# A streaming encoder step: the first layer norm written into TensorE's order among the last convolutions, the sums of both layer norms on VectorE, and the last two taps of a GpSimd convolution behind a gate

## The chip, the cores and the metric

The kernel runs on one core of a Trainium2 chip. The metric is the time of one execution on the device in microseconds (us). A core has five engines that each work through a fixed list of instructions in order: TensorE (PE in the profile, its weight loads PEld), VectorE (DVE), ScalarE (ACT), GpSimd (POOL) and SyncE (SP), which mostly issues DMAs. They wait for each other through semaphores. [...]

## The reference

One step of a small encoder for two groups of frames: 512 new frames of one stream and 16 new frames of each of 8 running streams, 640 columns together, with a model width of 1024. The first layer is a convolution module and a feed-forward network, the second an attention layer and a feed-forward network. The change lies in the convolution module:

```python
def layer_norm(x, g, b):
    xf = x.astype(jnp.float32)
    mu = jnp.mean(xf, axis=-1, keepdims=True)
    var = jnp.mean(jnp.square(xf - mu), axis=-1, keepdims=True)
    y = (xf - mu) * lax.rsqrt(var + EPS)
    return (y * g.astype(jnp.float32) + b.astype(jnp.float32)).astype(x.dtype)

def conv_module(h, hist, g, w_pw1, b_pw1, w_dw, b_dw, ln_g, ln_b, w_pw2, b_pw2):
    a, gate = jnp.split(rms_norm(h, g) @ w_pw1 + b_pw1, 2, axis=-1)
    glu = a * jax.nn.sigmoid(gate)
    full = jnp.concatenate([hist.astype(glu.dtype), glu], axis=1)
    y = lax.conv_general_dilated(full, w_dw[:, None, :], ..., feature_group_count=D_MODEL) + b_dw
    y = jax.nn.silu(layer_norm(y, ln_g, ln_b))
    return h + y @ w_pw2 + b_pw2, full[:, -CONV_HIST:]
```

The depthwise convolution has 31 taps. The layer norm takes its mean and its variance over the 1024 channels of each frame.

## The kernel before, in words

**Layout.** Channels lie on the 128 partitions in 8 blocks, frames in the free dimension: the 128 frames of the running streams first, then the 512 of the new one. The 640 columns are worked on as two groups of 320 (`g` is 0 or 1; `gr[g]` has start and width). Each matrix product is three matmuls with operands split into a rounded part and a rest (`mm3`, L179 to L181): weight-high by x-high, weight-low by x-high, weight-high by x-low. `wsplit` makes the weight parts (`whi` on ScalarE, L152, `wlo` on VectorE, L156), `xsplit` those of the operands (L168, L169).

**Order.** A string, `PLAN`, lists the steps of the module, and `step` emits each. A planner then puts every engine's instructions in order by priority and by modelled times, so that instructions of a later step can be put among those of an earlier one wherever they seem ready. `tc.issue_after(i)` ties the instructions emitted inside it that run on the engine of `i` to stand behind `i` on that engine; `tc.high_priority` raises priorities.

**The steps.** `a`, `b`, `c`, and the first half of `C` to `F` make the GLU of a channel block (`glu`, tanh at L717, the other half's copy at L720, the product on VectorE at L724 and L730). The convolutions of the eight blocks are spread over the engines. Step `q` (block 0, then block 3) is a GpSimd convolution of the new stream's 512 frames (`conv_pool`): for each of 31 taps ScalarE makes a product (`cvt`, L777, four buffers) and GpSimd adds it to `ca` (L780). Step `d` gives parts of blocks 0 to 2 to VectorE (`conv_taps`, L766 and L769), some of whose last taps are held for step `e`, behind E7's GLU. Blocks 4 to 7 are done by TensorE (`conv_pe`, L818) in three parts: `S` (the 128 frames), `A` (192 more, which with S fill group 0) and `B` (the 320 of group 1). A part is 8 tap groups of 4 matmuls; a matmul in plain float32 shows as two instructions in the trace, so a part has 64. Part B reads a copy of the data shifted by DMA (`xb`, two buffers, `conv_read`, L800); that of block 7 is read in step `L`. Each part ends in a copy from PSUM to `y` by ScalarE (`to_y`, L738); four PSUM banks (`mm`) go round among GLU halves and convolution parts. Step `k` copies the results of VectorE's and GpSimd's convolutions to `y`.

**The layer norms.** Step `n` is `conv_ln(g)`. The mean over channels is a matmul of each block of `y` with a column of 1/1024 (`colmean`, L216, three tiles of 128 frames, so 6 instructions an operand); the first `LCUT[g]` blocks are added first (on GpSimd, L207) into one operand. A small reduction (L220), a copy (L829) and a matmul (`spread`, L228) bring the mean back to all partitions; VectorE subtracts it from the eight blocks (L832), ScalarE squares them (L188, `sql`). The squares' mean goes the same way with `SQCUT[g]`: for group 0 all eight blocks go to TensorE, for group 1 GpSimd adds the eight first. EPS is added on VectorE (L250), the power -0.5 taken on GpSimd (L257), the result spread; VectorE multiplies (L841), ScalarE applies silu (L843), and `xsplit` makes the operands of `pw2`. Step `w` (`pw2`) is the last pointwise product, per group 4 pairs of output blocks with 24 matmuls an output. The feed-forward network (L404) follows.

Before, step `n0` stands ahead of `B5 L7 B6 B7` in the list and the planner mixes them on TensorE; `n1` stands behind.

Of the kernel before, what the change touches and what calls it, by code (L numbers as in the profile page):

```python
# [15 lines left out]
P = 128  # L16
# [7 lines left out]
T = 512  # L24
# [18 lines left out]
CUT, LCUT, SQCUT = 8, (5, 5), (1, 8)  # L43
# [25 lines left out]
        "S7 A7 n0 B5 L7 B6 B7 s0 n1 w0 w1")  # L69
# [9 lines left out]
def tile_trunk(ctx, tc, xT, vecs, hist, w_pw1, w_pw2, w_in0, w_out0, w_os0, w_in1, w_out1, w_os1,  # L79
# [96 lines left out]
    def mm3(ps, wts, xs):  # L176
        last = len(wts) - 1
        for i, ((wh, wl), (xh, xl)) in enumerate(zip(wts, xs)):
            nc.tensor.matmul(ps, wh, xh, start=(i == 0), stop=False)  # L179
            nc.tensor.matmul(ps, wl, xh, start=False, stop=False)  # L180
            end = nc.tensor.matmul(ps, wh, xl, start=False, stop=(i == last))  # L181
        return end
# [11 lines left out]
    def tiles(n):  # L194
        return [min(t, n - P) for t in range(0, n, P)]

    def colmean(st, pieces, n, cut, tag, eng=nc.gpsimd, accp=None):
# [15 lines left out]
        for k, f in enumerate(srcs):  # L213
            s = f()
            for t, a in enumerate(tiles(n)):
                nc.tensor.matmul(st[:, 512 + t * w + k:513 + t * w + k], s[:, a:a + P],  # L216
                                 onec, start=True, stop=True)
# [8 lines left out]
    def spread(st, r, n):  # L226
        for t, a in enumerate(tiles(n)):
            nc.tensor.matmul(st[:, a:a + P], r[:, t:t + 1].to_broadcast([P, P]), ident,  # L228
                             start=True, stop=True)
        return st[:, :n]  # L230
# [466 lines left out]
    glu_end, gate_end = [None], [None]  # L697
# [74 lines left out]
    def conv_pool(c):  # L772
        acc = cp.tile([P, T], F32, tag="ca", name=nm("ca"))
        for j in range(W):
# [6 lines left out]
        return lambda: to_y(c, NB * SB, T, acc, func=AF.Copy)  # L781
# [22 lines left out]
    def conv_pe(c, part):  # L804
# [3 lines left out]
        for tg in range(8):  # L808
            r = 96 if tg == 7 else P
            for q in range(4):  # L810
# [5 lines left out]
                else:  # L816
                    mv = xb[0:r, q, 4 * tg:4 * tg + n]
                nc.tensor.matmul(pt[32 * q:32 * q + 32, 0:n], w4[0:r, 4 * tg + q, :], mv,  # L818
                                 start=(tg == 0), stop=(tg == 7))
# [3 lines left out]
    def conv_ln(g):  # L823
# [3 lines left out]
        r, v = colmean(mu, [lambda c=c: y[g][:, c, :] for c in order], n, LCUT[g], "mst")  # L827
        if v is not r:
            nc.vector.tensor_copy(r[:, :len(tiles(n))], v)  # L829
        spread(mu, r, n)  # L830
        for c in order:
# [3 lines left out]
        bc, _ = rstd_bc([y[g][:, c, :] for c in order], n, SQ, SQCUT[g],  # L835
                        sqs=[sq[:, i, :] for i in range(KT)])
# [9 lines left out]
        return z  # L846

    def pw2(g, z):
        n = gr[g][1]
        for m2 in M2[g]:  # L850
# [3 lines left out]
            if m2 < 2:  # L854
                del pws[KT, m2]
            for i in range(2):
                m = 2 * m2 + i
                pt = mmt()
                mm3(pt[:, :n], [(wh[:, (i * 8 + k) * P:(i * 8 + k + 1) * P],
                                 wl[:, (i * 8 + k) * P:(i * 8 + k + 1) * P]) for k in range(KT)],  # L860
                    xk(z, range(KT)))
# [547 lines left out]
```

## Time and profile before

| | |
|---|---|
| runs | 1490.59, 1491.54, 1494.51 us |
| median | 1491.54 us |
| the profiled execution | 1494.89 us, its span 1493.1 us |
| mean granted TensorE clock | 0.988 |
| busy: TensorE, VectorE, ScalarE, GpSimd | 97%, 75%, 51%, 22% of the span |
| from the GLU of block 7 to the first pw2 matmul | 135.9 to 198.5 us |

The page lists busy times, groups of instructions and the chain that ended last. The timeline gives the start and the duration of each instruction or run of instructions, its engine, line, tiles and shape; a bracket says how long the engine was idle before it and who released it. In the windows the granted clock is 1.00 at full speed.

### The profile page before, as it was taken

The numbers are of one execution on the slowest core, as the hardware profiler recorded it, in microseconds if no ns is written. First come the engines' busy times: TensorE is split into PE (matmuls) and PEld (weight loads), VectorE is DVE, ScalarE is ACT, GpSimd is POOL, SyncE is SP. The second block draws the span as 40 slices with busy tenths as digits, with TensorE's granted clock in tenths as the row PEclk, the third lists the DMA queues.
The fourth block names the chain that finished last, engine by engine and source line by source line (L and its number), as shares of the span: only waits on it lengthen the run. The fifth ranks groups of instructions, "written<-read, shape, count | busy, mean of one in ns | idle before, by whom it ended". The sixth has DMA issues, their size and how long they took to land.

```text
span 1493.1 us, 28157 instructions
## 1 busy us (share of the span) xinstructions
PE 1443.9 (97%) x10998; PEld 1377.0 (92%) x10998; DVE 1125.9 (75%) x2494; ACT 757.4 (51%) x1620; POOL 325.5 (22%) x376
## 2 busy tenths in 40 slices
PE   5998999999999999999999999999999999999997
PEld 5997789999999999999988898878999999999997
DVE  5788546799788788766867668576788888788754
ACT  3666246464554554444655355443454455465443
POOL 5789322011111111013222111012001111111101
PEclk9999999999999999999999999999899999999998
DMA  7167514034544544424555554452024544544512
GB/s 238 67 169 199 117 57 140 31 101 121 156 110 118 153 112 116 145 86 157 195 175 193 178 193 163 142 186 78 29 75 118 148 117 115 151 117 108 157 58 71
DMA packets 66661, 192.57 MB, mean 129 GB/s; under 512 B 12000, under 2 KB 30176, under 8 KB 58080
## 3 DMA queue, kind: packets, MB, share of 16 engines
q1 hardware_dynamic: 52736, 161.10, 33.2%
q0 software_dynamic: 13504, 29.37, 9.7%
q8 instruction: 86, 1.41, 0.4%
q14 instruction: 47, 0.39, 0.1%
q10 hardware_dynamic: 288, 0.31, 0.1%
HBM read 179.14 MB, written 11.61 MB: 128 GB/s over the span
## 4 chain that ended last, share of the span: by engine, by line
PE 81%; POOL 6%; DVE 6%; ACT 4%; DMA 1%; issue 1%; POOLq 0%; DVEq 0%; ACTq 0%
PE mm L404 48%; PE mm L179 8%; PE mm L180 7%; PE mm L181 7%; POOL ca L780 5%; PE mm L818 2%; PE w L216 2%; PE am L1154 1%; PE w L1170 1%; PE am L1137 1%; ACT whi L144 1%; PE am L1201 1%; DVE wlo L338 1%; ACT whi L152 1%; DVE hid L558 1%
## 5 line engine op out<-in xcount | busy, mean ns | idle before, releaser
L404 PE MATMUL mm<-XH,whi 128*128 128x320 f32 x896 | 276.0, 311 | 1.1 <-ACT t L414 1.0
L404 PE MATMUL mm<-XH,wlo 128*128 128x320 f32 x896 | 277.0, 310 | 0.0
L404 PE MATMUL mm<-XL,whi 128*128 128x320 f32 x896 | 274.7, 309 | 0.0
L337 ACT ACTIVATE whi<-raw 128x512 fp32r<-128x512 f32 (+2 forms) x280 | 169.4, 613 | 146.2 <-PE mm L404 114.5
L179 PE MATMUL mm<-xh,whi 128*128 128x320 f32 (+2 forms) x640 | 201.0, 316 | 4.2 <-ACT xh L168 2.6
L338 DVE TENSOR_TENSOR wlo<-raw,whi 128x512 fp32r<-128x512 f32 (+2 forms) x280 | 184.9, 668 | 22.8 <-ACT whi L337 21.6
L180 PE MATMUL mm<-xh,wlo 128*128 128x320 f32 (+2 forms) x640 | 199.7, 313 | 0.6 <-DVE wlo L156 0.6
L181 PE MATMUL mm<-xl,whi 128*128 128x320 f32 (+2 forms) x640 | 196.8, 312 | 0.0
L404 PE MATMUL mm<-hid,whi 128*128 128x320 f32 x732 | 172.0, 310 | 2.9 <-DVE hid L338 2.6
L404 PEld LDWEIGHTS mm<-XH,whi 128*128 128x128 f32 x896 | 168.4, 189 | 2.1 <-ACT t L414 2.1
L404 PEld LDWEIGHTS mm<-XH,wlo 128*128 128x128 f32 x896 | 168.7, 188 | 0.0
L404 PEld LDWEIGHTS mm<-XL,whi 128*128 128x128 f32 x896 | 167.9, 188 | 0.0
L404 PEld LDWEIGHTS mm<-hid,whi 128*128 128x128 f32 x732 | 124.8, 188 | 5.8 <-DVE hid L338 3.7
L179 PEld LDWEIGHTS mm<-xh,whi 128*128 128x128 f32 x640 | 121.5, 190 | 7.4 <-ACT xh L168 3.1
L180 PEld LDWEIGHTS mm<-xh,wlo 128*128 128x128 f32 x640 | 121.7, 190 | 1.0 <-DVE wlo L156 0.8
L181 PEld LDWEIGHTS mm<-xl,whi 128*128 128x128 f32 x640 | 120.6, 189 | 0.4 <-issue 0.2
L404 PE MATMUL mm<-hid,wlo 128*128 128x320 f32 x366 | 112.9, 308 | 0.0
L404 PE MATMUL mm<-XH,shi 128*128 128x320 f32 x344 | 107.2, 312 | 3.2 <-ACT XH L337 3.2
L404 PE MATMUL mm<-XL,shi 128*128 128x320 f32 x344 | 106.8, 312 | 1.3 <-DVE XL L338 1.3
L404 PE MATMUL mm<-XH,slo 128*128 128x320 f32 x344 | 106.9, 311 | 0.0
L383 POOL DMA_DIRECT2D s<-in_w_in x38 | 22.0, 579 | 388.8 <-DVE wlo L338 208.6
L780 POOL TENSOR_TENSOR ca<-ca,cvt 128x512 f32<-128x512 f32 x60 | 91.4, 1524 | 15.0 <-ACT cvt L777 8.0
(245 smaller groups left out, 3389.1 us busy)
## 6 DMA issues: line engine op xcount, KB each, us to landing
raw<-in_w_in SPq DMA_DIRECT2D x38, 1024.0 KB
s<-in_w_in POOLq DMA_DIRECT2D x76, 256.0 KB, 4.2
raw<-in_w_os SPq DMA_DIRECT2D x24, 768.0 KB
cache<-in_ck SPq DMA_DIRECT2D x32, 512.0 KB
cache<-in_cv SPq DMA_DIRECT2D x32, 512.0 KB
raw<-in_w_pw SPq DMA_DIRECT2D x12, 1024.0 KB
s<-in_w_os POOLq DMA_DIRECT2D x48, 192.0 KB, 3.6
raw<-in_w_kq SPq DMA_DIRECT2D x8, 1024.0 KB
```

The lines of the kernel that those rows point to most:

```text
L144: nc.scalar.activation(out=hi[:, a:b], in_=raw[:, a:b], func=AF.Copy, scale=gain)
L152: nc.scalar.activation(out=hi[:, a:b], in_=raw[:, a:b], func=AF.Copy)
L179: nc.tensor.matmul(ps, wh, xh, start=(i == 0), stop=False)
L180: nc.tensor.matmul(ps, wl, xh, start=False, stop=False)
L181: end = nc.tensor.matmul(ps, wh, xl, start=False, stop=(i == last))
L216: nc.tensor.matmul(st[:, 512 + t * w + k:513 + t * w + k], s[:, a:a + P], onec, start=True, stop=True)
L337: nc.scalar.activation(out=hi, in_=src, func=AF.Copy)
L338: put_end[0] = nc.vector.tensor_tensor(out=lo, in0=src, in1=hi.bitcast(F32), op=sub).ins
L383: nc.gpsimd.dma_start(s1, src[:, 2 * n:3 * n])
L404: last = nc.tensor.matmul(pt, wt, v, start=(first and k == i == 0), stop=(k == n - 1 and i == 2), skip_group_check=True)
L780: nc.gpsimd.tensor_tensor(out=acc, in0=acc, in1=pr, op=ALU.add)
L818: nc.tensor.matmul(pt[32 * q:32 * q + 32, 0:n], w4[0:r, 4 * tg + q, :], mv, start=(tg == 0), stop=(tg == 7))
```

## The change

- **Order of the first layer norm.** Step `n` is now `staged_ln`. `conv_ln` has become a generator with stops, and `conv_pe` one that stops after each tap group. `staged_ln` runs them in turn, each tied behind the last TensorE instruction of the other: the mean behind A7; one tap group of B5; the spread of the mean, the subtractions, the squares and their sum; twelve tap groups (the rest of B5, the reading of block 7's copy, five of B6); the squares' mean; two tap groups; the spread of the power and the rest of the norm; then the nine groups left. Step `m` is the second layer norm.
- **Sums.** `LCUT` for group 0 goes from 5 to 7. The sums of the means of both norms are on VectorE instead of GpSimd; the squares of both norms are added into one operand on VectorE (before: none for group 0, on GpSimd for group 1). The second norm's mean sum is tied behind the first one's sum of squares on VectorE.
- **The gate.** Of the 31 taps of block 3's GpSimd convolution the last two (`QHELD`) are emitted in step `e`, their products on ScalarE tied behind the tanh of E7.
- **pw2.** The two outputs of a pair take their banks together, and for the first pair of group 0 the loop over the blocks of `z` is outside that over the two outputs.

```diff
-CUT, LCUT, SQCUT = 8, (5, 5), (1, 8)
+CUT, LCUT = 8, (7, 5)
+GAPS = 1, 12, 2
+QHELD = 2
-        "S7 A7 n0 B5 L7 B6 B7 s0 n1 w0 w1")
+        "S7 A7 n s0 m w0 w1")
...
+    def pool_taps(c, acc, js):
+        for j in js:
...
+    def conv_pool(c):
+        acc = cp.tile([P, T], F32, tag="ca", name=nm("ca"))
+        n = W - QHELD if c else W
+        pool_taps(c, acc, range(n))
+        return (lambda: to_y(c, NB * SB, T, acc, func=AF.Copy),
+                lambda: pool_taps(c, acc, range(n, W)))
...
-    def conv_ln(g):
+    def conv_ln(g, after=None):
         n = gr[g][1]
         mu = w2t()
         order = LNO[g]
-        r, v = colmean(mu, [lambda c=c: y[g][:, c, :] for c in order], n, LCUT[g], "mst")
+        with nullcontext() if after is None else tc.issue_after(after):
+            r, v = colmean(mu, [lambda c=c: y[g][:, c, :] for c in order], n, LCUT[g], "mst",
+                           nc.vector)
         if v is not r:
             nc.vector.tensor_copy(r[:, :len(tiles(n))], v)
-        spread(mu, r, n)
+        conv_end[0] = mean_end[0]
+        yield
+        end = spread(mu, r, n, True)
...
-        bc, _ = rstd_bc([y[g][:, c, :] for c in order], n, SQ, SQCUT[g],
-                        sqs=[sq[:, i, :] for i in range(KT)])
+        conv_end[0] = end
...
+            sum_end[0] = nc.vector.tensor_tensor(out=acc[:, :n], in0=prev, in1=s, op=ALU.add).ins
+            prev = acc[:, :n]
+        yield
+        r, v = colmean(st, [lambda: prev], n, 1, "rst", nc.vector)
...
+        nc.gpsimd.tensor_tensor(out=r2[:, :nt], in0=r[:, :nt], in1=mhalf[:, :nt], op=ALU.pow)
+        conv_end[0] = mean_end[0]
+        yield
+        conv_end[0] = spread(st, r2, n, True)
...
+    def last_convs():
+        yield from conv_pe(5, "B")
+        x4s[7][2] = x4s[7][2]()
+        yield from conv_pe(6, "B")
+        yield from conv_pe(7, "B")
+
+    def staged_ln():
+        ln, convs = conv_ln(0), last_convs()
+        for gap in GAPS + (None,):
+            with tc.issue_after(conv_end[0]):
+                next(ln, None)
+            with tc.issue_after(conv_end[0]):
+                for _ in convs if gap is None else range(gap):
+                    if gap is not None:
+                        next(convs)
...
+            pair = [mmt()[:, :n], mmt()[:, :n]]
+            both = m2 == M2[0][0] and g == 0
+            for ks in [range(k, k + 1) for k in range(KT)] if both else [range(KT)]:
+                for i in range(2):
+                    mm3(pair[i], [(wh[:, (i * 8 + k) * P:(i * 8 + k + 1) * P],
+                                   wl[:, (i * 8 + k) * P:(i * 8 + k + 1) * P]) for k in ks],
+                        xk(z, ks), ks[0] == 0, ks[-1] == KT - 1)
...
             with tc.issue_after(gate_end[0]):
                 conv_taps(held, {})
+            with tc.issue_after(glu_end[0]):
+                pool_rest.pop()()
```

More of the change, by code (lines that the diff above doesn't have):

```diff
@@ L224, in colmean, with spread @@
         return r, st[:, 512:512 + nt]
-    def spread(st, r, n):
+    def spread(st, r, n, ins=False):
         for t, a in enumerate(tiles(n)):
-            nc.tensor.matmul(st[:, a:a + P], r[:, t:t + 1].to_broadcast([P, P]), ident,
-                             start=True, stop=True)
-        return st[:, :n]
+            end = nc.tensor.matmul(st[:, a:a + P], r[:, t:t + 1].to_broadcast([P, P]), ident,
+                                   start=True, stop=True)
+        return end.ins if ins else st[:, :n]
     def rsqrt(y, v):
```

60 lines of the change are left out of this document (39 added, 21 removed).

## The prediction

> **What bounds the kernel now.** I read the page's busy row first, then the list of what TensorE waited for, then the timeline of TensorE between 118 and 221 us, then those of ScalarE, VectorE, GpSimd and the DMA queue beside it, and last the windows for the granted clock.
>
> ```profile
> span 1493.1 us, 28157 instructions
> PE 1443.9 (97%) x10998; PEld 1377.0 (92%) x10998; DVE 1125.9 (75%) x2494; ACT 757.4 (51%) x1620; POOL 325.5 (22%) x376
> ```
>
> TensorE is busy for 97% of the span, so the end moves by what TensorE is given less to do, by what it waits less, and by the clock at which it does it. All three occur between 143 and 221 us, and the change lies there.
>
> First place, the gate. Rows give start, duration, engine, line and count; the bracket is idle time and its releaser.
>
> ```profile
> 118.26 4.57 PE L818 MATMUL mm<-xa,w 128*32 128x128 f32 x128
> 131.45 4.52 PE L818 MATMUL mm<-xb,w 128*32 128x320 f32 x64
> 143.13 1.96 PE L818 MATMUL mm<-xa,w 128*32 128x128 f32 x64
> 148.09 4.14 PE L818 MATMUL mm<-xa,w 128*32 128x192 f32 x64 [3.00 <-ACT y L738]
> ```
> ```profile
> 141.92 1.32 ACT L777 ACTIVATE cvt<-gall,dwv 128x512 f32<-128x512 f32 x2
> 145.56 0.72 ACT L777 ACTIVATE cvt<-gall,dwv 128x512 f32<-128x512 f32 x1 [2.32 <-POOL ca L780]
> 146.90 0.72 ACT L777 ACTIVATE cvt<-gall,dwv 128x512 f32<-128x512 f32 x1 [0.62 <-POOL ca L780]
> 147.53 0.51 ACT L738 ACTIVATE y<-mm,vec 128x320 f32<-128x320 f32 x1
> ```
>
> The convolution of step B4 ran on TensorE at 131.45 and filled a PSUM bank. Its copy out of the bank (L738, 128x320) starts only at 147.53, since in ScalarE's fixed order it stands behind the last two tap products (L777) of the GpSimd convolution of channel block 3, and these wait for GpSimd to free a buffer. The four banks are full by 145.09 (B4, the two halves of E7, S5), so A5 waits 3.00 us.
>
> Second place, the clock. Columns: window, then busy time and count of PE, PEld, DVE, ACT and POOL, then the granted clock, DMA share and GB/s.
>
> ```profile
> 149.40:149.80 0.40, 0.40 (x16) 0.29 (x8) 0.40 (x1) 0.00 (x0) 0.40 (x1) 0.51 1.08 213
> 152.60:153.00 0.40, 0.40 (x4) 0.40 (x4) 0.40 (x3) 0.10 (x1) 0.32 (x2) 0.72 1.03 398
> 172.00:175.00 3.00, 3.00 (x39) 1.33 (x39) 1.03 (x2) 0.00 (x0) 1.13 (x2) 1.00 0.02 5
> 182.00:183.40 1.40, 1.40 (x15) 1.40 (x14) 0.00 (x0) 0.00 (x0) 0.00 (x0) 1.00 0.00 0
> 183.40:183.80 0.40, 0.40 (x5) 0.40 (x4) 0.00 (x0) 0.00 (x0) 0.00 (x0) 0.68 0.00 0
> 190.20:190.60 0.40, 0.40 (x10) 0.20 (x4) 0.00 (x0) 0.00 (x0) 0.00 (x0) 0.79 0.00 0
> ```
>
> The clock halves from 149.4 to 152.9 and from 183.5 to 190.4: once after the 3.00 us gap, once during a run of one-column matmuls.
>
> Third place, the first layer norm among the last convolutions:
>
> ```profile
> 168.53 0.83 PE L216 MATMUL w<-onec,acc 128*128 128x1 f32 x6
> 169.22 1.70 PE L216 MATMUL w<-onec,y 128*128 128x1 f32 x14
> 170.85 0.74 PE L818 MATMUL mm<-xb,w 128*32 128x320 f32 x6
> 171.52 0.60 PE L216 MATMUL w<-onec,y 128*128 128x1 f32 x4
> 172.06 2.89 PE L818 MATMUL mm<-xb,w 128*32 128x320 f32 x36
> 174.88 0.93 PE L228 MATMUL w<-ident,mst 128*128 128x128 f32 x6
> 175.74 3.44 PE L818 MATMUL mm<-xb,w 128*32 128x320 f32 x48
> 179.11 6.40 PE L216 MATMUL w<-onec,sql 128*128 128x1 f32 x48
> 185.44 5.84 PE L818 MATMUL mm<-xb,w 128*32 128x320 f32 x44
> 191.21 0.93 PE L228 MATMUL w<-ident,rst 128*128 128x128 f32 x6
> 192.07 4.50 PE L818 MATMUL mm<-xb,w 128*32 128x320 f32 x58
> 196.50 0.83 PE L216 MATMUL w<-onec,acc 128*128 128x1 f32 x6
> ...
> 219.25 0.83 PE L216 MATMUL w<-onec,acc 128*128 128x1 f32 x6 [0.80 <-POOL acc L207]
> ```
>
> No gap is marked from 168.53 to 218, yet 72 one-column matmuls (L216: 6+14+4+48) do sums that could be done elsewhere. The last three convolutions are the five L818 pieces, 192 instructions.
>
> **Term A, the gate.** The last two of 31 taps are emitted later and put on ScalarE behind E7's tanh, so nothing in that queue waits for GpSimd ahead of B4's copy. E7's matmuls end by 143.1 and S5's by 145.09, the two taps before them end at 143.24, so the copy can be done by 143.8 and the bank is free before A5 asks. That removes 3.00 us of idle time. A5 at the half clock took 4.14 us; a pair of an S and an A part takes 4.57 and an S part 1.96, so A alone 2.61, and 1.53 us go too. What is late next: E7's tanh comes some 4 us earlier with all that hangs on it (the copies of block 7, F7), and GpSimd still ends its three last adds near where they end now; their result is read only after F7's tanh. Term A: -4.5 us. If the copy is still queued behind the taps, it is 0.
>
> [...]
>
> **Term B, fewer one-column matmuls.** Means: from four operands (a sum of five and three single blocks, 24 instructions) to two (a sum of seven and one, 12). Squares: from eight operands (48) to one (6). From the starts, 48 took 185.44-179.11 = 6.33 us, 0.132 each; the first 20 took 2.32 us, 0.116 each. So 42 x 0.132 = 5.54 and 12 x 0.116 = 1.39. Term B: -6.9 us. For the second layer norm the counts stay.
>
> **Term C, clock in the convolutions.** The five pieces took, start to next start, 0.67+2.82+3.37+5.77+4.43 = 17.06 us; at B4's 4.52/64 = 0.0706 each, 192 take 13.56. The difference lies in the piece at 185.44, run at half clock after the 48. With 6 in their place I take it as gone: -3.5 us.
>
> **Term D.** The 0.80 us at 218.2 is a wait for GpSimd's sum of the second layer norm's squares. That goes to VectorE. Term D: -0.8 us.
>
> **Term E, what the written order adds.** TensorE may run nothing else while it waits, and behind each wait stand the convolutions B5 to B7 and then the first pw2. The rows for the length of each chain:
>
> ```profile
> 151.49 9.95 DVE L769 SCALAR_TENSOR_TENSOR w<-gall,dwv,w 128x128 f32<-128x128 f32 x32
> ...
> 162.21 2.29 DVE L156 TENSOR_TENSOR wlo<-raw,whi 128x2048 fp32r<-128x2048 f32 x1 [0.37 <-ACT whi L152]
> ...
> 172.37 0.86 DVE L829 COPY mst<-mst 128x3 f32<-128x3 f32 x1
> 175.92 3.27 DVE L832 TENSOR_TENSOR y<-y,w 128x320 f32<-128x320 f32 x8 [2.69 <-PE w L228]
> ...
> 201.93 0.17 DVE L829 COPY mst<-mst 128x3 f32<-128x3 f32 x1
> ```
> ```profile
> L207 DVE TENSOR_TENSOR acc<-acc,sq x20: 481/493/559, 6.8 to 1050.6; 128x320 f32<-128x320 f32 x14, 128x384 f32<-128x384 f32 x6
> ```
> ```profile
> 186.01 0.86 POOL L257 TENSOR_TENSOR rst<-rst,mhalf 128x3 f32<-128x3 f32 x1 [12.81 <-DVE rst L250]
> ```
> ```profile
> 199.36 1.18 ACT L168 ACTIVATE xh<-cvt 128x320 fp32r<-128x320 f32 x3
> ```
> ```profile
> 198.76 0.31 PE L180 MATMUL mm<-xh,wlo 128*128 128x320 f32 x1
> 198.91 0.31 PE L181 MATMUL mm<-xl,whi 128*128 128x320 f32 x1
> ```
> ```profile
> 177.61 1.74 SPq L800 DMA_DIRECT2D xb<-sb  x4
> ```
>
> Times here are on the old axis, with A7's end at 168.53.
> - First mean. VectorE has the held taps until 161.4 and a weight split until 164.5, then six adds of 0.49 us, done by 167.5: before A7 ends. No wait; bounds 0 to 1.
> - Mean to spread: a reduce and a copy. The copy took 0.17 us in one place and 0.86 in the other, beside a GpSimd add. With no adds on GpSimd I take 0.17, a chain of some 0.6 us; the one tap group in between (8 x 0.0706 = 0.56) covers it. Bounds 0 to 0.8, taken 0.3.
> - Squares: eight subtractions (3.27) and seven adds (7 x 0.41 to 7 x 0.49, by the subtractions' spacing and by the row) make 6.1 to 6.7 us on VectorE, with 0.3 for the first and last hand-over; 12 groups cover 96 x 0.0706 = 6.78. Bounds 0 to 0.6, taken 0.2.
> - Power and spread: 0.17 and 0.86 us with hand-overs, 1.3; two groups cover 1.13. Taken 0.2, bounds 0 to 0.6.
> - pw2. The last normalized block (L168) is ready at 200.54, 8.4 us after the spread's end near 192.1, the eight being made one after another. After the spread come 72 instructions, 5.1 us, and then pairs of outputs with the blocks outermost: 6 matmuls a block, which start 0.15 apart, 0.9 us, so block 7 is wanted 5.1+7 x 0.9 = 11.4 us after the spread. No wait; bounds 0 to 1.
> - B7's shifted copies (SP queue) are issued when B5's buffer is free, 177.61, and from 182.0 on the DMA share is 0.00, 4.7 us after B5 ends (22 of the 48 instructions after 175.74, so 177.3). In the new order B6's 64 instructions (4.52 us) and 1.9 us of one-column matmuls, wait and spread lie between B5's end and B7's start: 6.4 us. Covered, with 1.7 us to spare.
>
> The 24 adds on VectorE, 12 us in all, lie in a stretch where it idles (1.03 of 3 us busy from 172, nothing from 182 to 183.4, in the windows above). GpSimd is left with the powers. The second norm's chain loses GpSimd's adds, so the second pw2 has its operands earlier than now. Term E: 0.7 for the three waits and 0.3 for the places without one, +1.0 us; bounds 0 to 4, none below nothing because no gap is marked there today.
>
> **Sum.** -4.5-6.9-3.5-0.8+1.0 = -14.7 us. The profiled execution took 1494.89 us, 1.8 more than its span, and lies 3.35 above the median of 1491.54. 1494.9-14.7 = 1480.2, less 3.35 gives 1476.8; I say 1477. After 221 us nothing is edited and TensorE is nearly full, so the gain should pass to the end.
>
> **Rivals.**
> 1. *The clock drops lie otherwise.* The run that sets the median may lack the drop at A5 (1.5 us not to be gained), and the new start of the norm may make one: 1.4 us of one-column matmuls, a wait and a spread in 3.2 us hold only 0.56 us of convolution. A drop of 3.4 us at half speed costs 1.7. For it: that stretch is thin. Against it: 168.53 to 172.06 is as thin today (0.67 us of convolution in 3.5) and the clock from 172 to 175 is 1.00. Time: 1477+3.2 = 1480. [...]
> 2. *The hold frees nothing:* B4's copy stays behind the taps, or A5 waits for another bank. Term A is lost: 1477+4.5 = 1481.5. Against: E7's tanh cannot run before 143.1 and B4's matmuls end near 136, so a planned order has the copy ready 7 us before the tanh that the taps now follow.
> 3. *TensorE waits in its written order,* at the first mean: the sum of seven on VectorE comes late behind held taps and weight split, and B5 to B7, 13.56 us that today fill such waits, stand behind it. Each us late costs one. From 10.2 us late the change is within 0.3% of no change (4.5 us, about what a measurement of this kernel can tell), from 14.7+4.5 = 19.2 us it is slower; 22 us late gives 1499. Against: by the rows the sum is ready a microsecond before A7 ends.
>
> **How the numbers follow.** Forecast 0.62, rival 1 0.14, rival 2 0.10, rival 3 0.14 (0.06 in its middle stretch, 0.08 slower). Range: low 1477 less the 1.0 of term E, less 4 for the spread of the runs and a clock drop elsewhere that may be missing (1490.59 to 1494.51 is 3.9): 1472; one more for term C, whose pieces also change over less often: 1471. High: rival 2 with term E at its bound: 1481.5+3 = 1484.5, say 1485. Faster 0.86, same 0.06, slower 0.08.
>
> **What would show it.** A5 starts right behind S5, with no bracket, at a clock of 1.00; the copy of B4 ends before 145; L216 in the first norm has 12 and 6 instructions; the convolutions B5 to B7 add up to 13.6 us; from A7's end to the first pw2 matmul some 18 us instead of 30, or 21 with the second norm's mean ahead of it; no wait over 1 us for VectorE or GpSimd in the norm. I am wrong if a bracket of several us stands at L216 or L228 behind A7, if A5 still waits, or if the gain is there at 250 us and gone at the end.

## The result, and the profile after

| | before | after |
|---|---|---|
| median of 20 runs each | 1494.21 us (1490.59 to 1500.27) | 1491.88 us (1484.97 to 1495.29) |
| ratio, 95% interval | | 0.9974 (0.9962 to 0.9986) |
| the profiled execution (span) | 1494.89 (1493.1) us | 1484.97 (1483.1) us |
| mean granted TensorE clock in it | 0.988 | 0.993 |
| end of A7 | 168.53 us | 168.62 us |
| first pw2 matmul | 198.53 us | 189.08 us |
| end of the last add of pw2 | 262.33 us | 257.10 us |

The change takes 0.26% off the time, 3.9 us of 1494 (by the ratio; the two medians differ by 2.3 us), where 14.7 were forecast; both the forecast 1477 and its range to 1485 lie below the median. The profiled execution of the kernel after is the fastest of its 20, so its span is not the one to explain: 10.0 us shorter, of which 5.2 are there by the end of pw2 and 4.8 come later, where nothing was edited. The last section returns to those. "The end of pw2" below is the end of the last add on VectorE (`h<-mm`); both kernels have the same work behind it.

The page's busy row of the kernel after:

```profile
PE 1429.6 (96%) x10944; PEld 1366.3 (92%) x10944; DVE 1136.4 (77%) x2517; ACT 757.5 (51%) x1620; POOL 307.1 (21%) x361
```

TensorE has 54 instructions fewer (10998 before), the 42 and 12 that were counted. Now its timeline between the gate and the first pw2 product:

```profile
142.63 4.56 PE L827 MATMUL mm<-xa,w 128*32 128x128 f32 x128
154.35 4.57 PE L827 MATMUL mm<-xa,w 128*32 128x128 f32 x128
162.88 5.80 PE L827 MATMUL mm<-xa,w 128*32 128x128 f32 x128 [3.97 <-DMA xa<-sa]
168.62 0.83 PE L220 MATMUL w<-onec,acc 128*128 128x1 f32 x6
169.31 0.81 PE L220 MATMUL w<-onec,y 128*128 128x1 f32 x6
170.05 0.74 PE L827 MATMUL mm<-xb,w 128*32 128x320 f32 x8
170.72 0.94 PE L232 MATMUL w<-ident,mst 128*128 128x128 f32 x6
171.59 6.68 PE L827 MATMUL mm<-xb,w 128*32 128x320 f32 x96
179.00 0.83 PE L220 MATMUL w<-onec,acc 128*128 128x1 f32 x6 [0.73 <-DVE acc L862]
179.76 1.28 PE L827 MATMUL mm<-xb,w 128*32 128x320 f32 x16
181.20 0.93 PE L232 MATMUL w<-ident,rst 128*128 128x128 f32 x6 [0.15 <-POOL rst L869]
182.06 5.06 PE L827 MATMUL mm<-xb,w 96*32 96x320 f32 x72
```
```profile
142.64 0.51 ACT L742 ACTIVATE y<-mm,vec 128x320 f32<-128x320 f32 x1
```

In its first row S5 and A5 run together, in 4.56 us: the gate's gap is gone, and B4's copy (ScalarE) stands at 142.64 where it stood at 147.53. S6 and A6 begin at 154.35, 5.3 us earlier than before (159.68). But S7, in the third row, now waits 3.97 us, for `xa`, the shifted copy of block 7 that comes by DMA, and then S7 and A7 take 5.80 us instead of 4.57. A7 ends where it ended before. From there the written order does what the forecast said: 18 one-column instructions, waits of 0.73 and 0.15 us, convolution pieces without a half-clock stretch, and the first pw2 matmul after 20.5 us instead of 30.0.

What TensorE waited for between 140 us and the end of pw2 (columns: us in total, times, longest) in the kernel after; before, the list had the 3.00 us of A5 and the 0.80 us at L216:

```profile
PE mm L827 <- DMA xa<-sa: 4.0, 1, 4.0
PE mm L181 <- ACT xh L170: 1.6, 1, 1.6
PE w L220 <- POOL acc L211: 0.7, 1, 0.7
PE w L220 <- DVE acc L862: 0.7, 1, 0.7
...
PE mm L181 <- DVE h L919: 0.5, 1, 0.5
...
```

(Left out are one of 0.7 us at the end of pw2, which stands in both, and one of 0.2.) The two waits that were to go are gone, and five others came; the two at L181 are at 223.29 and 224.95, where step `w1`, pw2 of the second group, asks for its operands. The clock stayed at half speed in two windows of this stage (162 to 165.5 and 189 to 193):

```profile
162.00:165.50 3.50, 2.62 (x52) 2.65 (x56) 0.36 (x1) 0.00 (x0) 0.00 (x0) 0.51 1.00 216
189.00:193.00 4.00, 4.00 (x18) 4.00 (x19) 1.76 (x5) 3.48 (x8) 0.00 (x0) 0.57 0.00 0
```

### The profile page after: what moved, and what is told of

It is laid out like the page before. It is cut to its first block, busy times and chain, and to the rows that moved or that the text cites. A ratio compares the mean times of both kernels' runs of the same rounds, so it can differ in the third digit from the quotient of the medians.

```text
span 1483.1 us, 28058 instructions
## 1 busy us (share of the span) xinstructions
PE 1429.6 (96%) x10944; PEld 1366.3 (92%) x10944; DVE 1136.4 (77%) x2517; ACT 757.5 (51%) x1620; POOL 307.1 (21%) x361
## 4 chain that ended last, share of the span: by engine, by line
PE 77%; DVE 8%; POOL 5%; ACT 4%; DMA 3%; issue 3%; POOLq 0%; SPq 0%; DVEq 0%; ACTq 0%
PE mm L408 44%; PE mm L181 8%; PE mm L182 8%; PE mm L183 8%; POOL ca L783 4%; PE mm L827 1%; PE w L220 1%; DVE wlo L342 1%; PE am L1220 1%; DMA raw<-in_w_os 1%; PE w L1236 1%; PE am L1203 1%; ACT whi L146 1%; PE am L1267 1%; DVE B L445 1%
## 5 line engine op out<-in xcount | busy, mean ns | idle before, releaser
L181 PE MATMUL mm<-xh,whi 128*128 128x320 f32 (+2 forms) x640 | 201.5, 317 | 6.3 <-ACT xh L170 4.2
L181 PEld LDWEIGHTS mm<-xh,whi 128*128 128x128 f32 x640 | 121.8, 191 | 9.7 <-ACT xh L170 5.0
```

What stands on the lines that cost most here:

```text
L181: nc.tensor.matmul(ps, wh, xh, start=(first and i == 0), stop=False)
```

## The experiments

A table of all, for comparison; each is told below. The half clock is the time at a granted clock near 0.5 between 143 us and the end of pw2, by windows of 0.5 us; "wait at S7" is that for `xa`.

| kernel | ratio (95%) | wait at S7 | A7 ends | pw2 ends | half clock |
|---|---|---|---|---|---|
| before | 1 | none | 168.53 | 262.33 | 10.2 |
| after | 0.9974 (0.9962 to 0.9986) | 3.97 | 168.62 | 257.10 | 6.8 |
| after, again | 0.9965 (0.9950 to 0.9980) | 4.74 | 170.94 | 257.90 | 6.8 |
| after without hold | 0.9962 (0.9946 to 0.9978) | none | 168.33 | 258.38 | 10.2 |
| before with hold | 1.0000 (0.9985 to 1.0016) | 5.87 | 171.01 | 264.73 | 13.6 |
| before with the sums | 0.9949 (0.9931 to 0.9967) | none | 168.34 | 255.47 | 10.2 |
| no copy for block 7 | 0.9919 (0.9896 to 0.9942) | none | 164.13 | 252.55 | 3.4 |
| third load late | 0.9940 (0.9919 to 0.9962) | 1.36 | 166.95 | 255.46 | 3.4 |
| fourth load late | 0.9972 (0.9956 to 0.9989) | 3.92 | 169.93 | 256.85 | 6.8 |
| both loads late | 0.9971 (0.9956 to 0.9987) | 1.80 | 165.90 | 257.37 | 10.2 |
| split low | 0.9969 (0.9951 to 0.9987) | 5.33 | 171.50 | 260.18 | 13.6 |
| second norm staged | 0.9956 (0.9940 to 0.9972) | 3.72 | 168.72 | 253.79 | 6.8 |
| the same, third load late | 0.9931 (0.9905 to 0.9956) | 3.41 | 168.93 | 254.00 | 6.8 |
| S7's wait filled | 0.9927 (0.9903 to 0.9950) | 3.31 | 171.55 | 252.19 | 3.4 |
| all of these | 0.9922 (0.9900 to 0.9944) | 0.72 | 168.83 | 253.57 | 6.8 |

In the last two kernels A7's end has 48 instructions of B5, 3.4 us, ahead of it that stand behind it in the others.

Each ratio is to runs of the kernel before taken beside that kernel, so times of two rows are not to be subtracted from each other. By the intervals only the kernel without the copy, S7's wait filled, and all of these lie below both rows of the kernel after (they reach 0.9950 at most). For the others the three times of the table speak, and each is from one profiled execution.

**The kernel after, again, and without the hold.**

> The changed kernel once more, for a second profile. In its first profile TensorE waited 3.97 us at S7 for the shifted copy of block 7 and the half clock lasted 20.4 us in all (3.4 at S7, 3.4 at 189, 6.8 near 1046, 6.8 at the end), against 36.3 us before. Theory Q (the gate's gain is lost again at S7, a DMA wait): the wait at S7 is there again, 3 to 5 us, and the last add of the last pointwise product ends near 257.1 us. Theory C (the small measured gain is mostly where the half clock happens to fall): the wait is there too, but the stretch around 1040 to 1061 us has another number of half-clock windows (3.4 us each) than the 6.8 us of the first profile, and the time moves with it by half of the difference. Rival M (the written order costs several us that the first profile happened not to show): waits of over 1 us at the means or spreads of the first norm.

> The changed kernel with no tap held (the gate undone, the rest kept). Theory Q: A5 waits 3 us again as before, S7 no longer waits, and the last add of the last pointwise product ends within 1 us of the changed kernel's 257.1; the time is within 0.1% of the changed kernel's. Rival M (the gate is worth its 4.5 us): the last add ends near 261.5 and the time is 4 to 5 us longer than the changed kernel's.

```diff
-QHELD = 2
+QHELD = 0
```

Measured: 1490.83 and 1490.28 us, ratios 0.9965 and 0.9962. Without the hold, A5 waits 3.00 us again, and S7 not at all; with it, the reverse (first row the kernel without the hold, second the kernel after, again):

```profile
147.81 4.37 PE L827 MATMUL mm<-xa,w 128*32 128x192 f32 x64 [3.00 <-ACT y L742]
```
```profile
163.83 7.11 PE L827 MATMUL mm<-xa,w 128*32 128x128 f32 x128 [4.74 <-DMA xa<-sa]
```

What follows: the hold frees A5 as forecast, and the time does not show it. The end of pw2 at 258.38 us without it is 1.3 and 0.5 us later than in the two profiles with it; 4.5 was the forecast.

**The hold alone, on the kernel before.**

> The kernel before with the two taps held, nothing else changed. Theory Q: the 3.00 us wait of A5 is gone, a wait of 3 to 5 us for the shifted copy of block 7 stands at S7 instead, and the last add ends within 1 us of the 262.3 of before. Rival M: no wait at S7 and the last add ends near 257.8.

```diff
+QHELD = 2
...
-        for j in range(W):
+    def pool_taps(c, acc, js):
+        for j in js:
...
+            with tc.issue_after(glu_end[0]):
+                pool_rest.pop()()
```

Measured: 1495.61 us, ratio 1.0000. The gap at A5 is gone, and S7 is late:

```profile
164.59 6.42 PE L824 MATMUL mm<-xa,w 128*32 128x128 f32 x128 [5.87 <-DMA xa<-sa]
```

A7 ends 2.5 us later than before. What the hold gives at A5 is taken back, and a little more, at S7, with or without the rest of the change.

**The sums alone, on the kernel before: no written order, no hold.**

> The kernel before with the sums alone changed: seven and one operands for the first mean, one for the squares, all these sums on VectorE; TensorE's order left to the planner, no tap held. Theory S (the gain of the norm is the 54 one-column matmuls and the half clock behind them, 6.9 and 3.5 us): from A7's end to the first matmul of the last pointwise product about 20 us as in the changed kernel (20.5), and the last add ends within 1.5 us of 257.5. Theory W (the written order carries part of it): the planner's order leaves waits or comes to the first pointwise matmul more than 2 us later, and the last add ends at 259.5 or later.

```diff
-CUT, LCUT, SQCUT = 8, (5, 5), (1, 8)
+CUT, LCUT, SQCUT = 8, (7, 5), (8, 8)
...
-        r, v = colmean(..., n, LCUT[g], "mst")
+        r, v = colmean(..., n, LCUT[g], "mst", nc.vector)
...
-        bc, _ = rstd_bc([y[g][:, c, :] for c in order], n, SQ, SQCUT[g],
+        bc, _ = rstd_bc([y[g][:, c, :] for c in order], n, SQ, SQCUT[g], eng=nc.vector,
```

Measured: 1486.18 us, ratio 0.9949, pw2's end 6.9 us earlier than before. That is 1.6 us more than the whole change brings by the end of pw2; the intervals of the two ratios overlap. It is term B and term D together (the second norm's squares are on VectorE here too, and GpSimd's wait of 0.80 us is gone), less 1.0 us of new waits (0.69 and 0.31). Term C brings nothing here: the clock falls as often as before, only elsewhere, where 24 one-column instructions now stand in a row ahead of the first pw2 matmul.

```profile
187.63 0.80 PE L216 MATMUL w<-onec,acc 128*128 128x1 f32 x6
188.29 2.91 PE L216 MATMUL w<-onec,y 128*128 128x1 f32 x18
...
190.00:196.00 6.00, 6.00 (x24) 6.00 (x25) 4.34 (x13) 5.53 (x13) 0.00 (x0) 0.50 0.00 0
```

No wait stands at `w1` in this kernel: VectorE has its second norm's last spread at 217.70, in the kernel after at 221.16. So beside the sums the rest of the change lost time. The kernel after without the hold comes to its first pw2 matmul 2.3 us earlier (188.73 for 191.07), and ends pw2 2.9 us later (258.38 for 255.47).

**No copy for block 7.**

> The changed kernel without block 7's shifted copy: S7 and A7 read the copy of block 6, so block 7's convolution for group 0 is left out in effect, and the write to DRAM and the four reads (1.5 MB) are not made. It shows what the wait at S7 is worth. Theory Q: no wait at S7, no half clock behind it, S6 to A7 follow each other in 9.1 us, and the last add of the last pointwise product ends 4.7 to 7 us earlier than in the two profiles of the changed kernel (257.1 and 257.9), near 251 to 252.5. Rival: the second norm's chain ends at the same time anyway and the second pointwise product waits for it, so that less than 2 us come through.

```diff
-                x4s[c] = [w4, conv_shift(c, "a", 0, NSC if op == "D" else NXA), None]
+                x4s[c] = [w4, x4s[6][1] if c == 7 else
+                          conv_shift(c, "a", 0, NSC if op == "D" else NXA), None]
```

Measured: 1482.23 us, ratio 0.9919. S6 to A7 run in one piece of 8.94 us, A7 ends 4.5 us earlier and pw2 4.6 us earlier than in the kernel after. So the copy is what holds the gate's gain back, and nothing else stands behind it: with it out of the way all of term A arrives at the end.

```profile
155.19 8.94 PE L827 MATMUL mm<-xa,w 128*32 128x128 f32 x256
```

**What makes the copy late.** Before, S6 to A7 ran in one piece:

```profile
159.68 8.92 PE L818 MATMUL mm<-xa,w 128*32 128x128 f32 x256
```

S7 is its second half, from 164.1 us. The copy that it reads is one write of the GLU's result to memory (`sa<-gall`) and four shifted reads (`xa<-sa`). SP's issues, before, then after (start, duration, what is issued, count):

```profile
144.42 0.35 SPq L141 DMA_DIRECT2D raw<-in_w_pw  x1
144.88 2.12 SPq L800 DMA_DIRECT2D xb<-sb  x4
...
151.60 0.34 SPq L794 DMA_DIRECT2D sa<-gall  x1
155.10 1.74 SPq L800 DMA_DIRECT2D xa<-sa  x4
161.86 0.34 SPq L794 DMA_DIRECT2D sb<-gall  x1
...
164.53 0.36 SPq L141 DMA_DIRECT2D raw<-in_w_pw  x1
```
```profile
143.91 0.35 SPq L143 DMA_DIRECT2D raw<-in_w_pw  x1
144.89 1.79 SPq L809 DMA_DIRECT2D xb<-sb  x4
...
147.25 0.38 SPq L803 DMA_DIRECT2D sa<-gall  x1
154.30 1.74 SPq L809 DMA_DIRECT2D xa<-sa  x4
157.09 0.34 SPq L803 DMA_DIRECT2D sb<-gall  x1
...
159.29 0.36 SPq L143 DMA_DIRECT2D raw<-in_w_pw  x1
```

The gate brings the write forward by 4.4 us, but the reads, which wait for it, by 0.8: the write now has a 1 MB weight load and the shifted reads of block 6 ahead of it, which start within 0.6 us of where they started before, and takes 7.0 us instead of 3.5. The gate also brings the next weight load forward, from 164.53 to 159.29, and the write of block 7's other copy (`sb`, 175 KB) from 161.86 to 157.09, among the reads. Either load could be the cause, or neither. Three kernels moved the loads.

> The changed kernel with one DMA moved on its queue: the 1 MB load of the third pair of weights of the last pointwise product, issued at 143.9 us and used from 199 us on, is tied behind the four reads of block 7's shifted copy. No other engine's order changes. Theory Q: 1 MB at the some 210 GB/s of that stretch is 5 us, so the copy lands up to 5 us earlier, the 3.97 us wait at S7 is gone or under 0.5 us with the half clock behind it, and the last add ends near 252 to 253 us; the time falls by 4 to 5 us. Rival L (the copy is bound by its own round trip through DRAM, not by what is ahead of it): the wait stays within 1 us of 3.97 and the time does not move.

```diff
+                with tc.issue_after(read_end[0]) if m2 == 2 else nullcontext():
+                    pws[KT, m2] = wsplit(w_pw2[m2], 16, P, pool=PL2[g])
```

> The kernel after with one issue on SP's queue moved: the 1 MB load of the fourth pw2 weight pair, issued at 159.29 in the kernel after, goes behind the reads of B7's shifted copy (175.63). All other instructions keep their order. Theory (the gate also brings this load forward, from 164.53 to 159.29, into the time of the copy's reads): the reads take from issue to the end of the burst what they take without the gate, 155.10 to 162.0 or 6.9 us, so S7 starts near 161.2, its wait falls from 3.97 and 4.74 us to 2.3, and the last add of the last pointwise product ends between 254 and 256 (257.1 and 257.9 in the two profiles of the kernel after). Rival (the copy's round trip alone is that long): S7 starts at 162.9 or later, the wait stays at 4 to 5 us and the add ends at 257 to 258.

> As the run before, and the 1 MB load of the third pair (143.91 in the kernel after) goes there too, so that no weight load lies before or among the writing and reading of block 7's copy. Theory: the write, issued near 147.3, lands in some 4 us instead of 7, the reads go out near 152 and end near 159, S7 waits 0 to 0.7 us, A7 ends near 164, and the last add of the last pointwise product ends at 252 to 253.5, as where block 7 made no copy (252.55). Rival: the end of the reads moves only by what the write moves in the run where the third pair's load alone was moved (wait 1.4 to 2.3 us, the add's end 255.5).

```diff
+            with tc.issue_after(read_end[0]) if g == 0 and m2 == 3 else nullcontext():
+                pws[KT, m2] = pws.get((KT, m2)) or wsplit(w_pw2[m2], 16, P, pool=PL2[g])
```

(In the third kernel `m2 > 1`.) Measured: ratios 0.9940, 0.9972 and 0.9971; the waits, in that order:

```profile
161.05 1.95 PE L829 MATMUL mm<-xa,w 128*32 128x128 f32 x62 [1.36 <-DMA xa<-sa]
```
```profile
162.67 7.26 PE L827 MATMUL mm<-xa,w 128*32 128x128 f32 x128 [3.92 <-DMA xa<-sa]
```
```profile
161.33 4.57 PE L827 MATMUL mm<-xa,w 128*32 128x128 f32 x128 [1.80 <-DMA xa<-sa]
```

The fourth pair's load falls out as a cause: with it gone from behind the reads the wait is still 3.92 us. The third pair's load is a part: without it ahead of the write the wait is 2.6 us shorter in one pair of kernels (3.97 to 1.36) and 2.1 in the other (3.92 to 1.80). In both pairs 0.8 us of that is A6 ending later; S7 starts 1.8 and 1.3 us earlier. With the third load late, another 0.96 us is lost in a gap inside S7 and A7 for which the profile names no wait. The rest of the wait is mostly the copy's own length, as two stretches of the kernel with the fourth load late show (DMA share and GB/s stand last):

```profile
153.00:155.00 2.00, 2.00 (x41) 1.81 (x43) 1.81 (x6) 0.65 (x2) 0.65 (x1) 1.00 0.06 9
155.20:162.00 6.80, 3.55 (x100) 2.74 (x91) 6.45 (x12) 3.65 (x9) 0.00 (x0) 0.96 1.02 216
```

The DMA engines are nearly empty from 153 to 155 (share 0.06, 9 GB/s), between the write's data and the reads' data, then full for 6.8 us (share 1.02, 216 GB/s); of the 1.47 MB moved there the four reads are 1.2. With both loads away the write is issued at 149.16, the reads at 153.29, and S7 starts at 161.33: 12.2 us in all, and none of these kernels shortens the last 8. The `sb` write is not what makes them 8: with the third load late it is issued behind that load, and S7 still starts 8.2 us after the reads' issue (152.87 to 161.05). What the 2 us from 153 to 155 are spent on is not shown. Both loads late ends pw2 no earlier than the kernel after although A7 ends 2.7 us earlier: its clock halves for 6.83 us between 238 and 245, which costs 3.4 (the window's granted clock is 0.51). My expectation of 252 to 253.5 there was wrong for both reasons; the 252 to 253 for the third load alone was missed too (255.46).

```profile
238.00:245.00 7.00, 7.00 (x30) 7.00 (x30) 4.24 (x6) 3.28 (x5) 1.25 (x1) 0.51 0.70 235
```

**The waits at `w1`.**

> The changed kernel with one priority lowered: the split of the third pair of weights of the last pointwise product (1.9 us on ScalarE, 2.3 on VectorE) is no longer raised, so that the planner may put the second norm's squares and their sums ahead of it. In the changed kernel the split stands between the first and the second square (199.45) and again ahead of the sums (202.66), and the sums end at 212.4, against 207.4 in the kernel with the sums alone. Theory Z (this is why the second pointwise product waits at 223 to 225): the squares run in one piece, the sums end 2 us or more earlier, the waits of 1.58 and 0.52 us shrink to under 1 us in all, and the last add ends at 254.5 to 256. Rival: the planner places the spread of the power where its model has it, whatever the chain does on the chip, and the last add stays within 1 us.

```diff
-        with tc.high_priority(offset=HP):
+        with tc.high_priority(offset=prio):
...
-                pws[KT, m2] = wsplit(w_pw2[m2], 16, P, pool=PL2[g])
+                pws[KT, m2] = wsplit(w_pw2[m2], 16, P, pool=PL2[g],
+                                      prio=0 if m2 == 2 else HP)
```

Measured: 1491.29 us, ratio 0.9969. The squares of the second norm still stand one before and seven after the weight split on ScalarE (second row, 204.07), and the wait is the same 1.58 us; the edit did not move what it was to move, so it does not test the theory of the split's priority.

```profile
201.88 0.48 ACT L190 ACTIVATE sql<-y 128x320 f32<-128x320 f32 x1 [6.58 <-DVE y L846]
204.07 2.62 ACT L190 ACTIVATE sql<-y 128x320 f32<-128x320 f32 x7
...
226.10 0.41 PE L181 MATMUL mm<-xh,whi 128*128 128x320 f32 x1 [1.58 <-ACT xh L170]
```

The rival fits: what sets the wait is the place that the planner gives the spread of the power among the 192 matmuls of `w0`. Counted in the timelines (a record or two may be missing), it stands behind 188 of them in the kernel after, in its repeat, without the hold and without the copy, and behind 187 here. In these kernels `w1` waits 1.58 and 0.52 us. It stands behind 153 before and behind 150 with the sums alone, and there `w1` does not wait. The data were there earlier: in the kernel after the sum of the squares ends on VectorE at 212.4 us and its mean stands at 215.66 on TensorE; EPS is added at 216.49 and the spread stands at 220.29, none of them with a wait.

> The changed kernel with the second norm also in written order, among the outputs of the first group's pointwise product: its mean after seven blocks of the first pair, the spread of the mean one block later, the squares' mean three outputs on, the spread of the power one output later; and the second mean summed to one operand (6 one-column matmuls instead of 24). Theory Z (2 to 3 us are lost in the changed kernel because the planner places the second norm's matmuls some 3 us after their data each time, so that the second pointwise product waits for its operands): the waits at 223 to 225 us (1.58 and 0.52) are gone, 18 one-column matmuls (2.1 us) and the half clock at 189 too, and the last add ends 4 to 6 us earlier, at 252 to 253.5. Rival: the written order makes as many waits at its own places, over 1 us each, and the last add moves by less than 2 us.

> The last two together: second norm in written order and the weight load behind block 7's reads. If the two losses are separate the gains add: the last add ends near 250.5 (257.5, less 5 for the second norm, less 2 for the load, as measured with the load alone: 255.46), and the time is 6 to 7 us below the changed kernel's and 10 to 12 below that of the kernel before. If one hides the other, the last add is where the better of the two alone has it.

```diff
-CUT, LCUT = 8, (7, 5)
+CUT, LCUT = 8, (7, 8)
+GAPS2 = 7, 1, 3, 1
...
+    def staged_pw2():
+        ln, prod = conv_ln(1, sum_end[0]), pw2(0, zs[0])
+        for gap in GAPS2 + (None,):
...
```

Measured: 1487.74 and 1484.49 us, ratios 0.9956 and 0.9931. With the second norm's matmuls written among those of `w0` no wait is left at `w1` (the spread stands behind 144 of the 192), and pw2 ends 3.3 us earlier than in the kernel after, not the 4 to 6 expected; a half clock stands at 210 to 213.5 instead of 189 to 193, and a wait of 2.17 us for the sum of its squares takes part of it back, since I had put that one too early:

```profile
208.46 0.83 PE L221 MATMUL w<-onec,acc 128*128 128x1 f32 x6 [2.17 <-DVE acc L863]
```

Adding the late third load here moved S7's wait by only 0.3 us (3.41 us), not by the 2.6 that it was worth alone, and the end of pw2 not at all: 254.00, where 250.5 was expected if the gains add. The write of the copy was issued at 149.85 there, not at 147.25 as in the kernel after, and S7 started at 162.71; why the write came later is not shown.

**S7's wait filled, and all together.**

> The changed kernel with the first six of the eight tap groups of B5 put on TensorE between A6 and S7, where the changed kernel waits some 4 us for block 7's shifted copy; the written order of the norm keeps its gaps (1, 12, 2 groups) and has 3 groups left at the end instead of 9. Theory Q (the gate's gain was lost only because nothing was there to run until the copy lands): 48 instructions, 3.4 us, fill the wait; what is left at S7 is under 1 us with no half clock behind it; A7 ends at the same time as in the changed kernel (168.6) although six groups more are done; the first pointwise product comes 2 to 3 us earlier (it may wait up to 1 us for its first block), and the last add ends at 253.5 to 256. Rival (the second norm's chain sets the end of the second pointwise product): TensorE is earlier at the first pointwise product but waits longer at the second one, and the last add stays within 1 us of 257.1 to 257.9.

> All that helped together: six groups of B5 ahead of S7, the second norm in written order (its squares' mean half an output later than in the run with that order alone, where it waited 2.17 us), one operand for its mean, the weight load behind block 7's reads. If the losses are separate: no wait over 1 us at S7, none over 1 us at the second norm's squares, and the last add ends 2 to 4 us before that of the second norm's written order (253.8): at 250 to 252; the time is 12 to 14 us below that of the kernel before, a ratio of 0.991 to 0.992. If one of them hides another: 253 or later, and a ratio no better than the 0.9931 of the last two together.

```diff
+EARLY = 6
...
-        "S7 A7 n s0 m w0 w1")
+        "P S7 A7 n s0 m w0 w1")
...
+        elif op == "P":
+            with tc.issue_after(conv_end[0]):
+                for _ in range(EARLY):
+                    next(conv_rest)
```

(The second kernel has the two edits above as well, with `GAPS2 = 7, 1, 7, 1` and pw2's outputs of `w0` in halves.) Measured: 1483.77 and 1483.74 us, ratios 0.9927 and 0.9922. Six tap groups of B5 run while the copy is on its way (first row), and S7 still waits (second), yet pw2 ends 4.9 us earlier than in the kernel after. That gain is not the filled gap's. The copy landed later in this profile (S7 at 165.44 for 162.88), B7 waits 1.26 us for its own copy (third row), and the first pw2 matmul comes at 189.38, in the kernel after at 189.08. The gain lies behind it: in this kernel the planner has put the spread of the second norm's power behind 153 of `w0`'s matmuls (fourth row), in the kernel after behind 188 (last row), and the waits of 1.58, 0.52 and 0.75 us are gone, as is the half clock at 189 to 193 (1.7 us), 4.6 us together. What filling the gap is worth by itself is not shown. With the second norm staged and the third load late as well, S7 waits 0.72 us, but 6.83 us of half clock fell at 171.5 to 178.5, and pw2 ends at 253.57, where 250 to 252 was expected; the two kernels can't be told apart by their times. Both beat the kernel before, and the kernel after too, below whose interval (0.9962 to 0.9986) theirs lie.

```profile
158.71 3.42 PE L828 MATMUL mm<-xb,w 128*32 128x320 f32 x48
...
165.44 6.11 PE L828 MATMUL mm<-xa,w 128*32 128x128 f32 x128 [3.31 <-DMA xa<-sa]
...
180.77 1.82 PE L828 MATMUL mm<-xb,w 128*32 128x320 f32 x24 [1.26 <-DMA xb<-sb]
...
213.91 0.83 PE L233 MATMUL w<-ident,rst 128*128 128x128 f32 x6
```
```profile
220.29 0.83 PE L232 MATMUL w<-ident,rst 128*128 128x128 f32 x6
```

## Why the prediction was wrong, step by step

- **Term A (-4.5): the step that failed.** A5's gap and half clock went, as said, and the F7 and block 7 work came some 5 us earlier. The step "What is late next: E7's tanh comes some 4 us earlier with all that hangs on it (the copies of block 7, F7)" named the right things and priced them at nothing. Of SP's queue I used only the row of B7's copy. The write at 151.60, the reads at 155.10 and S7 at 164.1 were in the trace of before: a chain of up to 12.5 us with its end close ahead of S7 (the DMA engines fell idle at 162.0). Moved forward by 4.4 us, its write met a full queue (DMA share 0.95 to 1.07 from 146 to 152, the write 7.0 us instead of 3.5), and A7 ended where it had. Measured: 0 (the hold alone 1.0000; the kernel after without it no slower).
- **Term B (-6.9): right, its exact size by luck.** 54 instructions are gone, and the sums alone end pw2 6.9 us earlier, but with term D's 0.8 and 1.0 us of new waits in it. The price of 0.132 us was read from 48 matmuls that ran at half clock from 183.5 on; the first 20, at full clock, took 0.116, by which the term is 6.3 and 0.7 us of it belongs to term C.
- **Term C (-3.5): right at its place, not in the sum.** The pieces of B5 to B7 now take 0.67+6.68+1.29+4.99 = 13.6 us. (Of the 3.5, the piece at 185.44 held 5.77-44 x 0.0706 = 2.7, not all; the rest lay in the other four.) But I booked a lost half-clock stretch as gone; the clock halved again for 3.41 us at the wait of S7, from 162.07 (1.2 us at S7 and A7, 5.80 for 4.57), and for 3.41 us behind 18 one-column matmuls, from 189.38 (1.7 us at 189 to 193). In the repeated profile both lay at S7 (granted clock 0.54 from 162 to 165.5 and 0.55 from 165.5 to 169.5). Rival 1 allowed for such drops, with a chance of 0.14; the 3.4 us of a drop in it is the length measured before (3.41 us, from 149.40), and its price of 3.2 us is near the 2.9 that they cost, but it looked for one at the norm's start, where none fell (granted clock 1.00 from 168.6 to 187).
- **Term D (-0.8): right and outdone.** GpSimd's wait is gone, and "the second pw2 has its operands earlier than now" holds (the spread of the power comes at 220.29 for 224.13), but not early enough, and "After 221 us nothing is edited" overlooked that step: `w1` waits 1.58 and 0.52 us where it waited for nothing, and 0.75 us more stand at 239.56. TensorE reaches `w1` 9 us earlier by way of the first norm (221.7 for 230.5), and the second norm's chain, whose matmuls the planner places, came forward by 3.8 (behind 188 of `w0`'s matmuls for 153). Writing that chain into TensorE's order took the two waits away.
- **Term E (+1.0): right in the sum, by luck in its parts.** 0.73+0.15 = 0.9 us of waits; the 0.73 at the squares lies over the bound of 0.6 that was set for it, and the spread of the mean, taken at 0.3, did not wait. The first pw2 matmul came 20.5 us after A7, for which 21 was named.

The sum as measured, to the end of pw2: -14.7, +4.6 for term A (A7 0.1 us later instead of 4.5 earlier), +1.7 for the clock at 189, +2.1 at `w1` and +0.75 at 239.56 give -5.5; the row says -5.2. The drop at S7 is inside the 4.6.

**The base.** I took 3.35 us off for the distance of the profiled execution from the median of three runs, 1491.54. Over 20 runs the median is 1494.21: 2.7 us of the miss are that; the profiled execution lay only 0.7 above it.

**The rivals.** Rival 2 named the term that was lost (1481.5), but by another mechanism: the hold does free the bank. Rival 3 did not occur: no wait over 1 us stands in the first norm. The last way to be wrong, a gain that is there early and gone later, came nearest; but the gate's gain was gone by 168 us, and not between 250 us and the end.

**Open.** The copy's landing moved between 161.0 and 165.4 us among the profiles with the hold, with the same queue ahead of it in several; S7 starts 8.0 to 10.3 us after the reads' issue. Moving the loads explains a part. What moves the rest is open, and so are the worth of filling S7's gap and the reason why the planner places the spread of the power so differently.

## What to carry to other kernels

Before booking the removal of a wait, follow the data of the step that comes earlier through every DMA queue up to its next reader: if that chain now ends just ahead of its reader, its length bounds the gain. Here the gain came through where the chain was gone; that work put into the gap brings it home was not shown. When one chain comes forward, look where the next one's instructions stand in the fixed order: here 188 of 192 matmuls were ahead of the one that the next step waited for. A half-clock stretch that an edit removes should not be booked as gone from the sum: here 10.2 us of it between 143 us and the end of pw2 became 6.8, in other places. Take the base from many runs, and compare two profiles at a point behind the edit rather than by their spans.

## What the runs showed of the hardware

**The half clock moves, in units of 3.41 us, and the spread of the runs goes with it.** By windows of 0.2 us the clock was halved in the kernel before for 3.41 us from 149.40 and for 6.83 us from 183.54, in the kernel after for 3.41 us from 162.07 and from 189.38. In the stretch from 1030 to 1064 us, which no kernel edits, nine of the profiles show 2 to 5 such units; the windows before, after, and after again (the granted clock is the third column from the end):

```profile
1030.00:1064.00 34.00, 29.82 (x160) 28.99 (x160) 23.91 (x55) 13.52 (x27) 7.40 (x6) 0.75 0.32 99
```
```profile
1030.00:1064.00 34.00, 28.50 (x182) 27.81 (x181) 26.86 (x66) 18.45 (x38) 2.80 (x3) 0.90 0.23 81
```
```profile
1030.00:1064.00 34.00, 28.51 (x171) 27.83 (x170) 25.32 (x61) 16.60 (x34) 4.56 (x3) 0.85 0.29 93
```

Mean clocks of 0.75, 0.90 and 0.85 make 17.0, 6.8 and 10.2 us of the 34 at half clock: 5, 2 and 3 units. From before to after, 26.1 us at half clock behind the end of pw2 become 13.6; 12.5 us less are worth some 6 us, and the span gained 4.8 there. The 20 runs of the kernel after go the same way, from 1484.97 us at a mean clock of 0.993 to 1495.29 at 0.987. What makes the clock fall is not shown: in the kernel before it fell at 149.40, 1.3 us after the wait of 3.00 us had ended, and at 183.54, while 48 one-column matmuls kept TensorE busy from 179.11 to 185.44 us.

**A copy through memory is a long chain.** Shifting block 7's 295 KB by one write and four reads took 12.2 us at the least, from the write's issue to S7, in the kernels where S7 waited for it, with 216 GB/s moved while the reads ran. In the kernel before, where S7 did not wait, the data had moved 10.4 us after the write's issue (151.60 to 162.0).
